# SSD mixer: the decays' differences on ScalarE, and SiLU as (1 + tanh(x/2)) x/2 ending in the projection's PSUM bank

## The chip, the core and the metric

The kernel runs on one core of a Trainium2 chip. The metric is the device time of one execution in microseconds, as a median of several runs. The profile is one further execution. Engines are called PE (TensorE), PEld (TensorE's weight loads), DVE (VectorE), ACT (ScalarE), POOL (GpSimd) and SP (SyncE, which here only issues DMAs). Each runs its own instructions in order; semaphores join them.

## The reference, cut to what matters

The program is a two-layer decoder of 1040 tokens (16 of them learned) and width 1024: a Mamba-2 mixer, a convolution network, a stick-breaking attention and a second convolution network. Only the mixer is changed:

```python
z, xbc, dt_raw = split(u @ w_in)                 # 2048, 2048 + 2*4*128, 32 columns
xbc = silu(causal_dwconv(xbc, conv_w, conv_b))   # 4 taps
xs, b_in, c_in = split(xbc)
dt = softplus(dt_raw + dt_bias);  a = -exp(a_log)
a_cs = cumsum(dt * a)                            # within a chunk
decay_in = exp(where(causal, a_cs[l] - a_cs[s], -inf))
y_diag = einsum(c_c, b_c, decay_in, x_c * dt)    # within a chunk
y_off  = einsum(c_c, state, exp(a_cs))           # from the state before it
y = y_diag + y_off + xs * d_skip
hg = rmsnorm_per_group(y * silu(z)) * gate_g
out = hg @ w_out
```

There are 4 groups of 8 heads with 64 columns each, and a state of 128. All is float32; a product is made of three matmuls of rounded parts (high × high, high × low, low × high: lines L156, L157, L158).

## The kernel before

**Tiles.** Channels lie on the 128 partitions, tokens along the free axis. The 1040 tokens are projected in three tiles j = 0, 1, 2 of 348, 348 and 344. A *block* is 128 columns of w_in. A projection tile is 24 matmuls (8 blocks of u, three parts each) into one PSUM bank `pj`: j = 0 and 1 rotate through the two banks of the pool mm, j = 2 has a bank of its own, `ex`, which the dt projection `dtr` also uses at the start. Three more banks are the pool sm (cb, pb, y, ms, and the small products of the dt path), two are the pool lg (px, S).

**A tile of xbc** (`in_block`, with `conv`): ACT makes the first tap from `pj` with weight and bias (L278), DVE adds three taps (L282, each reads `pj` and `xbc`), ACT applies Silu in SBUF (L465). The Silu isn't issued at once: it is put on the list `open`, which `settle` empties behind the next tile's L278. `pj` is free after the third tap.

**A tile of the gate** (`gate_group`): ACT applies Silu from `pj` to `z` (L497), and `pj` is free; DVE multiplies it into the rows y, which stand in the tiles named `xbc` (L504); ACT squares (L509, through `open`); DVE adds the squares of the group's four blocks (L513, L515). `gate_norm` then sums over partitions with a matmul (`ms`, L189), takes ln and exp on ACT (L192, L193, with a table load L180 ahead), refines on DVE (L194 to L197) and scales the four rows (L526). Where it runs, ACT changes its function table: natural logarithm and exp share one, Silu is in another.

**The loop of chunks.** The prologue (0 to about 112 us) transposes x, makes dt and projects group 0's six blocks; its order on the engines is set by the build's scheduler, from its own costs. From there to about 690 us the order is written out by hand. Each of 4 groups runs 9 chunks of 116 tokens (the last has 112). A chunk is: `ssd_front` (matmuls cb, px and pb; DVE masks cb into cbm, L601, makes xdt, L603, and multiplies the decays by cbm, L604; ACT copies bk, L610; POOL makes xde, L612); two to four projection tiles of blocks that come later; and `ssd_back` (matmuls S, L625, and y, L637 and L639; DVE adds the state, L632, and the four rows of y, L641, which frees y's bank). Groups 0 and 3 have 18 tiles to spread over 9 chunks, groups 1 and 2 have 30. These tiles are group g+1's inputs and group g's gate, and the norms of group g's gate stand between the tiles of the block behind it.

**The decays** (`ssd_decays`) run one step ahead, between a chunk's projection tiles: a DMA on SP's queue broadcasts the cumulated sums of 8 heads into D; DVE makes 8 instructions min(a_cs[l] − a_cs[s], 0), one for each head with its own column as scalar (L579); ACT takes the exp of all (L580); POOL scales the state's factors E by c (L583). The sums come from `dt_path`: ACT copies `dtr` (L401), transposes, softplus on DVE (a reciprocal, L418, and a series), cumulation by a matmul, a copy of the rows (L448) and DMAs to memory (L452), which D's DMA (L568) reads back.

Of the kernel before, what the change touches and what calls it, by code (L numbers as in the profile page):

```python
# [10 lines left out]
AF = mybir.ActivationFunctionType  # L11
ALU = mybir.AluOpType
# [10 lines left out]
TT = [(0, 348), (348, 348), (696, 344)]  # L23
TW = 352
QW = 1056
HALO = 4
# [43 lines left out]
class Trunk:  # L70
    def __init__(self, ctx, tc, a):
        self.tc, self.nc, self.a = tc, tc.nc, a
        nc = self.nc
        self.cp = ctx.enter_context(tc.tile_pool(name="cp", bufs=1))
        self.qp = ctx.enter_context(tc.tile_pool(name="qp", bufs=NQ))
        self.tmps = ctx.enter_context(tc.tile_pool(name="up", bufs=8))
        self.wp = ctx.enter_context(tc.tile_pool(name="wp", bufs=3))
        self.mp = ctx.enter_context(tc.tile_pool(name="mp", bufs=2, space=bass.MemoryType.PSUM))
        self.sp = ctx.enter_context(tc.tile_pool(name="sp", bufs=SMB, space=bass.MemoryType.PSUM))
        self.dp = ctx.enter_context(tc.tile_pool(name="dp", bufs=1, space=bass.MemoryType.DRAM))  # L80
        self.n = 0
        self.open = []
        self.consts()


# [29 lines left out]
    def consts(self):  # L115
        nc, cp = self.nc, self.cp
        self.params = cp.tile([P, NPAR], F32, tag="params", name="params")
        nc.gpsimd.dma_start(self.params, self.a["params"])
        self.ident = cp.tile([P, P], F32, tag="ident", name="ident")
        nc.gpsimd.memset(self.ident, 0.0)  # L120
        nc.gpsimd.affine_select(out=self.ident, in_=self.ident, compare_op=ALU.not_equal, fill=1.0, base=0,
                                pattern=[[-1, P]], channel_multiplier=1)
        self.one = cp.tile([P, 1], F32, tag="one", name="one")
        nc.vector.memset(self.one, 1.0)
        self.ones = cp.tile([P, P], F32, tag="ones", name="ones")
        nc.vector.memset(self.ones, 1.0)
        self.eps = cp.tile([P, 1], F32, tag="eps", name="eps")
        nc.vector.memset(self.eps, EPS)
        self.zero = cp.tile([P, HALO], F32, tag="zero", name="zero")
        nc.vector.memset(self.zero, 0.0)  # L130

        self.past = cp.tile([P, CB], F32, tag="past", name="past")
        nc.gpsimd.memset(self.past, 1.0)
        nc.gpsimd.affine_select(out=self.past, in_=self.past, compare_op=ALU.is_ge, fill=0.0, base=0,
                                pattern=[[1, CB]], channel_multiplier=-1)
# [135 lines left out]
            self.mm3(ps[:m, : halo + n], w[0][:, k * m : k * m + m], w[1][:, k * m : k * m + m], hi[:, o:e], lo[:, o:e], k == 0, k == kb - 1)  # L271
        return ps

    def conv(self, ps, out, n, taps, halo, wcol, bcol, between=lambda: None, last=None):

        nc = self.nc
        o = halo - taps + 1
        nc.scalar.activation(out, ps[:, o : o + n], AF.Identity, scale=wcol(0), bias=bcol)  # L278
        between()
        for i in range(1, taps):  # L280
            to = out if last is None or i + 1 < taps else last
            nc.vector.scalar_tensor_tensor(to, ps[:, o + i : o + i + n], wcol(i), out, op0=ALU.mult, op1=ALU.add)  # L282


    def load_x(self, pool, mx):
# [65 lines left out]
        for step, j in ORD:  # L351
            (scaled if step else stream)(j)
# [103 lines left out]
    def in_block(self, u, col, cv, out):  # L456

        nc = self.nc

        def tile(w, j):  # L460
            s0, n = TT[j]
            ps = self.project(w, u, j, HALO, bank=self.ex if j == 2 else None)
            t = out[0][:, s0 : s0 + n]
            self.conv(ps, t, n, 4, HALO, lambda i: self.par("ssd_conv_w", cv * 4 + i), self.par("ssd_conv_b", cv), self.settle)
            self.open.append(lambda: nc.scalar.activation(t, t, AF.Silu))  # L465

        return self.a["w_in"][col // P], tile

# [18 lines left out]
    def gate_group(self, u, g, x, acc, later):  # L487

        nc = self.nc
        tt = nc.vector.tensor_tensor  # L490

        def block(q):
            def tile(w, j):
                s0, n = TT[j]
                ps = self.project(w, u, j, 0, bank=self.ex if j == 2 else None)
                z = self.tmp("z")
                nc.scalar.activation(z[:, :n], ps[:, :n], AF.Silu)  # L497
                self.settle()
                later(j, lambda: product(j, z))

            def product(j, z):
                s0, n = TT[j]
                xq = x[q][:, s0 : s0 + n]
                tt(xq, xq, z[:, :n], op=ALU.mult)  # L504
                self.open.append(lambda: square(j, z))

            def square(j, z):
                s0, n = TT[j]
                nc.scalar.activation(z[:, :n], x[q][:, s0 : s0 + n], AF.Square)  # L509
                if q == 0:  # L510
                    acc[j] = z
                elif q == 1:
                    nc.vector.scalar_tensor_tensor(acc[j][:, :n], acc[j][:, :n], EPS * (DI // GROUPS) / P, z[:, :n], op0=ALU.add, op1=ALU.add)  # L513
                else:
                    tt(acc[j][:, :n], acc[j][:, :n], z[:, :n], op=ALU.add)  # L515

            return self.a["w_in"][4 * g + q], tile

        return [block(q) for q in range(4)]
# [8 lines left out]
    def settle(self):  # L528

        todo, self.open = self.open, []  # L530
        for f in todo:
            f()

    def stream(self, blocks, w0=None):


        calls = {}
        todo = []
        for src, f in blocks:
            if src is None:  # L540
                for j in range(3):
                    calls[3 * len(todo) + 1 + j] = lambda f=f, j=j: f(j)
            else:
                todo.append((src, f))
        w = [w0 or self.load_w(todo[0][0], D)]
        for n in range(3 * len(todo)):
            i, j = divmod(n, 3)
            if j == 0:
                if i + 1 < len(todo):
                    w.append(self.load_w(todo[i + 1][0], D))  # L550
                cur = w.pop(0)
            if n in calls:
                calls.pop(n)()
            todo[i][1](cur, j)
            yield
        self.settle()
        for f in calls.values():
            f()

    def ssd_decays(self, g, ct, c, pool):  # L560

        nc = self.nc
        h0 = GH * g
        t0, n = CH[c]
        cc = 3 * (c % 3) + c // 3
        dk = pool.tile([P, 1024], F32, tag="D", name=self.nm("D"))
        dk = dk[:n, : GH * CB].rearrange("p (h l) -> p h l", h=GH)
        nc.sync.dma_start(dk, self.acs_d[c, h0 : h0 + GH].unsqueeze(0).to_broadcast([n, GH, CB]))  # L568
        dk = dk[:, :, :n]
        ce = None  # L570
        if c:
            ce = pool.tile([P, GH * CB], F32, tag="E", name=self.nm("E"), bufs=2)
            ce = ce.rearrange("p (h l) -> p h l", h=GH)
            nc.sync.dma_start(ce, self.ea_d[c, h0 : h0 + GH].unsqueeze(0).to_broadcast([P, GH, CB]))
            ce = ce[:, :, :n]
        yield dk, ce

        for i in range(GH):
            nc.vector.tensor_scalar(dk[:, i], dk[:, i], self.cols[:n, 1, cc, h0 + i : h0 + i + 1], 0.0, op0=ALU.subtract, op1=ALU.min)  # L579
        nc.scalar.activation(dk, dk, AF.Exp)  # L580
        yield
        if c:
            nc.gpsimd.tensor_tensor(ce, ce, ct[:, t0 : t0 + n].unsqueeze(1).to_broadcast([P, GH, n]), op=ALU.mult)  # L583
        yield
# [287 lines left out]
    def up(self, layer, w0, forms, rest, pool):  # L872
# [7 lines left out]
        def block(b, t, w):  # L880
# [683 lines left out]
```

## Time and profile before

| what | us |
|---|---|
| time, median of 3 runs (lowest to highest) | 3022.47 (3021.38 to 3026.99) |
| the profiled execution's own time | 3024.83 |
| its span, first to last instruction | 3023.1 |
| busy PE, DVE, ACT, POOL | 2875.1, 2158.8, 1621.9, 1403.3 |
| PE busy, 0 to 110 / 110 to 690 / the rest | 94.68 / 554.62 / 2225.85 |
| mean granted clock of PE | 0.981 |

A row of a group reads: line, engine, operation, output<-inputs, sizes, count, then busy us, mean ns of one, and the idle time of the engine just before them with what ended it. A row of the timeline reads: start, length, engine, line, operation, and in brackets the idle time before it. Times count from the span's start.

### The profile page before, as it was taken

Reading aid. Unit: us, or ns where it says so; the run is one execution under the profiler, and the core shown is the slowest. Engines: PE = TensorE matmul, PEld = TensorE weight load, DVE = VectorE, ACT = ScalarE, POOL = GpSimd, SP = SyncE. Lnnn points to the kernel's source line nnn. Section 1 sums busy time; section 2 is a strip of 40 time slices with the busy share of each in tenths; the row PEclk is TensorE's granted clock in tenths of the full one; section 3 lists DMA queues with packets and bytes.
Section 4 is the critical chain, followed back from the end, with each engine's and each line's share of the span. In section 5 each row is a group of like instructions: output and inputs, shape, how many; then the busy total and the mean of one; then the engine's idle time right before and its main releaser. Section 6 shows DMA issues by size and latency. Waiting matters only on the chain.

```text
span 3023.1 us, 57199 instructions
## 1 busy us (share of the span) xinstructions
PE 2875.1 (95%) x21855; PEld 2733.1 (90%) x21855; DVE 2158.8 (71%) x3994; ACT 1621.9 (54%) x3308; POOL 1403.3 (46%) x1282
## 2 busy tenths in 40 slices
PE   7999999989989999998999999999997999998988
PEld 4998998889979999998998999999797999997778
DVE  5686868875376665568966888888748665568895
ACT  4555555553245555554334888877735555554432
POOL 1254444532415666658733222222234676667751
PEclk9999999999999999999999999999998999999999
DMA  5243323313222222243132222221331222225231
GB/s 161 75 118 86 109 78 111 113 53 139 74 78 64 78 80 77 84 160 132 47 117 72 60 65 65 68 59 52 129 112 64 85 76 79 77 84 176 91 105 56
DMA packets 125891, 272.76 MB, mean 90 GB/s; under 512 B 15888, under 2 KB 55440, under 8 KB 125616
## 3 DMA queue, kind: packets, MB, share of 16 engines
q1 hardware_dynamic: 120304, 258.17, 27.1%
q10 hardware_dynamic: 4048, 6.36, 0.6%
q0 software_dynamic: 1264, 4.57, 0.4%
q8 instruction: 172, 2.82, 0.4%
q14 instruction: 103, 0.84, 0.1%
HBM read 200.93 MB, written 53.21 MB: 84 GB/s over the span
## 4 chain that ended last, share of the span: by engine, by line
PE 52%; DVE 13%; ACT 4%; issue 3%; DMA 2%; POOL 0%; SPq 0%; DVEq 0%; ACTq 0%; POOLq 0%
PE p L156 9%; PE p L157 9%; PE p L158 9%; PE acc L157 4%; PE acc L156 4%; PE acc L158 4%; DVE gl L1007 3%; PE po L1314 2%; PE pj L156 2%; PE pj L158 2%; PE pj L157 2%; PE lg L1272 1%; DVE kp L1285 1%; PE wT L1299 1%; ACT kp L1275 1%
## 5 line engine op out<-in xcount | busy, mean ns | idle before, releaser
L156 PE MATMUL pj<-uh,wh 128*128 128x348 f32 (+2 forms) x1536 | 507.3, 331 | 16.1 <-DVE qs L1223 7.1
L157 PE MATMUL pj<-ul,wh 128*128 128x348 f32 (+2 forms) x1536 | 498.7, 325 | 0.0
L158 PE MATMUL pj<-uh,wl 128*128 128x348 f32 (+2 forms) x1536 | 496.2, 323 | 0.0
L157 PE MATMUL p<-bl,fh 128*128 128x262 f32 (+1 forms) x1408 | 401.0, 285 | 14.0 <-DVE bl L827 14.0
L156 PE MATMUL p<-bh,fh 128*128 128x262 f32 (+1 forms) x1408 | 401.3, 286 | 4.2 <-ACT fh L858 3.5
L158 PE MATMUL p<-bh,fl 128*128 128x262 f32 (+1 forms) x1408 | 399.3, 284 | 0.0
L859 POOL TENSOR_TENSOR fl<-x,fh 128x1024 fp32r<-128x1024 f32 x88 | 212.7, 2418 | 306.4 <-ACT fh L858 277.5
L150 POOL TENSOR_TENSOR wl<-w,wh 128x1024 fp32r<-128x1024 f32 (+2 forms) x80 | 164.6, 2060 | 327.1 <-ACT wh L149 327.0
L156 PEld LDWEIGHTS pj<-uh,wh 128*128 128x128 f32 x1536 | 292.0, 190 | 23.8 <-DVE qs L1223 9.2
L157 PE MATMUL p<-bl,wh 128*128 128x262 f32 (+1 forms) x1056 | 301.8, 286 | 8.5 <-DVE bl L827 8.5
L156 PE MATMUL p<-bh,wh 128*128 128x262 f32 (+1 forms) x1056 | 301.9, 286 | 6.3 <-ACT bh L826 6.3
L158 PE MATMUL p<-bh,wl 128*128 128x262 f32 (+1 forms) x1056 | 301.2, 285 | 0.0
L157 PEld LDWEIGHTS pj<-ul,wh 128*128 128x128 f32 x1536 | 292.6, 190 | 1.4 <-issue 0.5
L158 PEld LDWEIGHTS pj<-uh,wl 128*128 128x128 f32 x1536 | 291.9, 190 | 0.3 <-issue 0.2
L157 PEld LDWEIGHTS p<-bl,fh 128*128 128x128 f32 x1408 | 268.0, 190 | 16.1 <-DVE bl L827 15.9
L282 DVE SCALAR_TENSOR_TENSOR c<-p,params,c 128x260 f32<-128x260 f32 (+1 forms) x440 | 207.9, 481 | 94.4 <-ACT c L278 92.6
L156 PEld LDWEIGHTS p<-bh,fh 128*128 128x128 f32 x1408 | 268.4, 191 | 6.0 <-ACT fh L858 3.9
L158 PEld LDWEIGHTS p<-bh,fl 128*128 128x128 f32 x1408 | 267.4, 190 | 0.1
L157 PE MATMUL acc<-gl,wh 128*128 128x260 f32 (+1 forms) x672 | 217.9, 326 | 19.8 <-DVE gl L1007 19.8
L909 DVE TENSOR_TENSOR p<-p,ft 128x262 f32<-128x262 f32 (+1 forms) x176 | 76.8, 436 | 221.6 <-ACT ft L906 128.9
L384 DVE TENSOR_TENSOR h<-h,acc 128x256 f32<-128x256 f32 (+4 forms) x232 | 102.6, 450 | 175.1 <-PE acc L158 172.5
L156 PE MATMUL acc<-gh,wh 128*128 128x260 f32 (+1 forms) x672 | 215.0, 325 | 8.7 <-DVE p L1054 5.4
(309 smaller groups left out, 8539.4 us busy)
## 6 DMA issues: line engine op xcount, KB each, us to landing
w<-in_w_up SPq DMA_DIRECT2D x88, 512.0 KB
w<-in_w_down SPq DMA_DIRECT2D x44, 512.0 KB
w<-in_w_in SPq DMA_DIRECT2D x40, 512.0 KB
E<-ea_d SPq DMA_DIRECT2D x32, 464.0 KB
D<-acs_d SPq DMA_DIRECT2D x32, 420.5 KB
g<-c SPq DMA_DIRECT2D x88, 130.0 KB
g<-c SPq DMA_DIRECT2D x88, 128.0 KB
b<-g SPq DMA_DIRECT2D x16, 520.0 KB
```

The lines of the kernel that those rows point to most:

```text
L150: nc.gpsimd.tensor_tensor(wl[:, :n], w32[:, :n], wh[:, :n].bitcast(F32), op=ALU.subtract)
L156: mm(out, wh, uh, start=first, stop=False, skip_group_check=joins)
L157: mm(out, wh, ul, start=False, stop=False, skip_group_check=joins)
L158: mm(out, wl, uh, start=False, stop=last, skip_group_check=joins)
L282: nc.vector.scalar_tensor_tensor(to, ps[:, o + i : o + i + n], wcol(i), out, op0=ALU.mult, op1=ALU.add)
L384: self.nc.vector.tensor_tensor(h[f][:, o], h[f][:, o], ps[:, :n], op=ALU.add)
L859: tt(lo[:, :n], t, hi[:, :n].bitcast(F32), op=ALU.subtract)
L909: add = lambda o, x, y: tt(o[:, :N], x[:, :N], y[:, :N], op=ALU.add)
L1007: tt(gl, x, gh.bitcast(F32), op=SUB)
L1272: nc.tensor.matmul(ps[:nt, :m], part[:, c0 : c0 + nt], ks[a][:, s0 : s0 + m], start=x == 0, stop=x == 1)
L1275: nc.scalar.activation(kp[:nt, :m], ps[:nt, :m], AF.Sigmoid, scale=self.rt[2][:nt, i : i + 1])
L1314: nc.tensor.matmul(po[64 * a : 64 * a + 64, w], v[: CH[c][1], c, 64 * a : 64 * a + 64], wt[a][: CH[c][1], c, :nt], start=x == 0, stop=x == ...
```

## The change

1. `ssd_decays`: the 8 DVE instructions become 8 ACT instructions Relu(a_cs[s] − a_cs[l]), with the head's column as bias and a scale of −1, and the exp takes a scale of −1. The value is the same.
2. SiLU becomes (1 + tanh(x/2)) · x/2. Tanh is in one table with exp. For xbc the halving is in the parameters: taps and biases of the convolution are multiplied by 0.5 once at the start (one DVE instruction). The last tap now writes back into the bank `pj`; ACT takes the tanh of it into a temporary; DVE makes (th + 1) · pj into the row. `pj` is free after that.
3. The gate: ACT takes tanh(z/2) from `pj`; DVE makes (th + 1) · pj into `pj` (for group 3 into the temporary); the product with the rows, with a factor of 0.5, reads it there. `pj` is free after the product, not after ACT.
4. A second list, `next`, holds DVE's SiLU step and the sums of squares; `follow` empties it behind the next tile's first tap.

```diff
@@ consts
+        halves = self.par("ssd_conv_b", 0, 24 + 24 * 4)
+        nc.vector.tensor_scalar(halves, halves, 0.5, None, op0=ALU.mult)
@@ conv
             nc.vector.scalar_tensor_tensor(to, ps[:, o + i : o + i + n], wcol(i), out, op0=ALU.mult, op1=ALU.add)
+            if i == 1:
+                behind()
@@ in_block
-            t = out[0][:, s0 : s0 + n]
-            self.conv(ps, t, n, 4, HALO, lambda i: self.par("ssd_conv_w", cv * 4 + i), self.par("ssd_conv_b", cv), self.settle)
-            self.open.append(lambda: nc.scalar.activation(t, t, AF.Silu))
+            t, y = out[0][:, s0 : s0 + n], ps[:, HALO : HALO + n]
+            self.conv(ps, t, n, 4, HALO, lambda i: self.par("ssd_conv_w", cv * 4 + i), self.par("ssd_conv_b", cv), self.settle, y, self.follow)
+
+            def silu():
+                th = self.tmp("th")[:, :n]
+                nc.scalar.activation(th, y, AF.Tanh)
+                self.next.append(lambda: nc.vector.scalar_tensor_tensor(t, th, 1.0, y, op0=ALU.add, op1=ALU.mult))
+
+            self.open.append(silu)
@@ gate_group
-                z = self.tmp("z")
-                nc.scalar.activation(z[:, :n], ps[:, :n], AF.Silu)
+                th = self.tmp("z")
+                nc.scalar.activation(th[:, :n], ps[:, :n], AF.Tanh, scale=0.5)
                 self.settle()
-                later(j, lambda: product(j, z))
+                self.follow()
+                z = th if g == 3 else ps
+                nc.vector.scalar_tensor_tensor(z[:, :n], th[:, :n], 1.0, ps[:, :n], op0=ALU.add, op1=ALU.mult)
+                later(j, lambda: product(j, z, th))
...
-                tt(xq, xq, z[:, :n], op=ALU.mult)
-                self.open.append(lambda: square(j, z))
+                nc.vector.scalar_tensor_tensor(xq, z[:, :n], 0.5, xq, op0=ALU.mult, op1=ALU.mult)
+                self.open.append(lambda: square(j, th))
...
                 nc.scalar.activation(z[:, :n], x[q][:, s0 : s0 + n], AF.Square)
+                self.next.append(lambda: add(j, z))
@@ ssd_decays
         for i in range(GH):
-            nc.vector.tensor_scalar(dk[:, i], dk[:, i], self.cols[:n, 1, cc, h0 + i : h0 + i + 1], 0.0, op0=ALU.subtract, op1=ALU.min)
-        nc.scalar.activation(dk, dk, AF.Exp)
+            nc.scalar.activation(dk[:, i], dk[:, i], AF.Relu, scale=-1.0, bias=self.cols[:n, 1, cc, h0 + i : h0 + i + 1])
+        nc.scalar.activation(dk, dk, AF.Exp, scale=-1.0)
```

In the changed kernel the lines are a little lower: the tap is L284, the tanh of xbc L472, its SiLU step L473, the taps' first step L280, Relu and exp L603 and L604, the gate norm's scaling L543. Three places show how the order moves; each row has the line, the operation and the tiles with their numbers.

DVE in the prologue, before: pj_596 is the first block's tile j = 2, in the bank `ex`, pj_728 the next tile that uses it. Rows from the reciprocal on:

```order
L418 RECIPROCAL dt_641<-dt_641 116x288
L282 SCALAR_TENSOR_TENSOR xbc_536<-pj_596,params,xbc_536 128x344
L419 TENSOR_TENSOR dt_642<-dt_640,dt_641 116x288
L282 SCALAR_TENSOR_TENSOR xbc_536<-pj_596,params,xbc_536 128x344
L282 SCALAR_TENSOR_TENSOR xbc_774<-pj_775,params,xbc_774 128x348
L420 TENSOR_TENSOR dt_640<-dt_642 116x288
L282 SCALAR_TENSOR_TENSOR xbc_536<-pj_596,params,xbc_536 128x344
L282 SCALAR_TENSOR_TENSOR xbc_774<-pj_775,params,xbc_774 128x348
```

The same place now; pj_599 and pj_737 are the two tiles, pj_673 and pj_705 the second block's other two:

```order
L422 RECIPROCAL dt_646<-dt_646 116x288
L284 SCALAR_TENSOR_TENSOR xbc_537<-pj_599,params,xbc_537 128x344
L423 TENSOR_TENSOR dt_647<-dt_645,dt_646 116x288
L284 SCALAR_TENSOR_TENSOR xbc_537<-pj_599,params,xbc_537 128x344
L284 SCALAR_TENSOR_TENSOR xbc_672<-pj_705,params,xbc_672 128x348
L424 TENSOR_TENSOR dt_645<-dt_647 116x288
L284 SCALAR_TENSOR_TENSOR pj_599<-pj_599,params,xbc_537 128x344
L284 SCALAR_TENSOR_TENSOR xbc_672<-pj_705,params,xbc_672 128x348
L425 TENSOR_SCALAR dt_646<-dt_645 116x288
L284 SCALAR_TENSOR_TENSOR pj_705<-pj_705,params,xbc_672 128x348
L473 SCALAR_TENSOR_TENSOR xbc_537<-th_699,pj_599 128x344
```

The last reader of the bank was a tap that stood six rows behind the reciprocal; now it is the SiLU step, ten rows behind it. On PE pj_728 came 39 matmuls of other tiles after pj_596's last; pj_737 comes 17 after pj_599's last.

ACT at the prologue's end, before, around the first chunk's decays:

```order
L278 ACTIVATE xbc_983<-pj_984,params 128x348
L465 ACTIVATE xbc_886<-xbc_886 128x348
L149 ACTIVATE wh_1076<-w_143_1074 128x1024
L580 ACT_TABLE_LOAD
L580 ACTIVATE D_1174<-D_1174 116x928
L278 ACTIVATE xbc_886<-pj_947,params 128x344
L465 ACT_TABLE_LOAD
L465 ACTIVATE xbc_983<-xbc_983 128x348
```

And now:

```order
L453 ACTIVATE ea_888<-rows_884 96x348
L472 ACTIVATE th_930<-pj_850 128x344
L280 ACTIVATE xbc_903<-pj_904,params 128x348
L603 ACTIVATE D_1211<-D_1211,cols 116x116 x8
L472 ACTIVATE th_962<-pj_904 128x348
L280 ACTIVATE xbc_903<-pj_936,params 128x348
L604 ACTIVATE D_1211<-D_1211 116x928
```

The Relus, which read D after its DMA, stand ahead of the tanh of pj_904, whose SiLU step frees its bank for pj_1007; before, only the exp stood there on ACT, and on DVE the differences stood ahead of the last tap of pj_984, which freed that tile's bank.

DVE in group 1's loop, at the end of the second norm of group 0's gate (its last two of eight steps), before: pj_2982 is the third tile of the block around it.

```order
L526 SCALAR_TENSOR_TENSOR xbc_774<-xbc_774,params,y_2971 128x348
L526 SCALAR_TENSOR_TENSOR xbc_886<-xbc_886,params,y_2971 128x348
L282 SCALAR_TENSOR_TENSOR xbc_2847<-pj_2982,params,xbc_2847 128x344 x3
L194 TENSOR_TENSOR z_2385<-y_3025 128x344
L195 TENSOR_TENSOR z_2385<-z_2385,ms_3023 128x344
```

And now; pj_2979 is that block's second tile, pj_3069 its third:

```order
L543 SCALAR_TENSOR_TENSOR xbc_785<-xbc_785,params,y_3058 128x348
L543 SCALAR_TENSOR_TENSOR xbc_903<-xbc_903,params,y_3058 128x348
L284 SCALAR_TENSOR_TENSOR xbc_2932<-pj_3069,params,xbc_2932 128x344
L473 SCALAR_TENSOR_TENSOR xbc_2932<-th_3095,pj_2979 128x348
L284 SCALAR_TENSOR_TENSOR xbc_2932<-pj_3069,params,xbc_2932 128x344
L284 SCALAR_TENSOR_TENSOR pj_3069<-pj_3069,params,xbc_2932 128x344
```

The SiLU step of the second tile, which frees its bank, stands behind the whole norm and the third tile's first tap; before, that bank was free after the tile's own third tap, ahead of the norm.

More of the change, by code (lines that the diff above doesn't have):

```diff
@@ L81, in __init__ @@
         self.n = 0
-        self.open = []
+        self.open, self.next = [], []
         self.consts()
@@ L272, in project, with conv @@
         return ps
-    def conv(self, ps, out, n, taps, halo, wcol, bcol, between=lambda: None, last=None):
+    def conv(self, ps, out, n, taps, halo, wcol, bcol, between=lambda: None, last=None, behind=lambda: None):
         nc = self.nc
@@ L495, in tile, with product @@
                 ps = self.project(w, u, j, 0, bank=self.ex if j == 2 else None)
-                z = self.tmp("z")
-                nc.scalar.activation(z[:, :n], ps[:, :n], AF.Silu)
+                th = self.tmp("z")
+                nc.scalar.activation(th[:, :n], ps[:, :n], AF.Tanh, scale=0.5)
                 self.settle()
-                later(j, lambda: product(j, z))
-            def product(j, z):
+                self.follow()
+                z = th if g == 3 else ps
+                nc.vector.scalar_tensor_tensor(z[:, :n], th[:, :n], 1.0, ps[:, :n], op0=ALU.add, op1=ALU.mult)
+                later(j, lambda: product(j, z, th))
+            def product(j, z, th):
                 s0, n = TT[j]
                 xq = x[q][:, s0 : s0 + n]
-                tt(xq, xq, z[:, :n], op=ALU.mult)
-                self.open.append(lambda: square(j, z))
+                nc.vector.scalar_tensor_tensor(xq, z[:, :n], 0.5, xq, op0=ALU.mult, op1=ALU.mult)
+                self.open.append(lambda: square(j, th))
             def square(j, z):
@@ L509, in square, with add @@
                 nc.scalar.activation(z[:, :n], x[q][:, s0 : s0 + n], AF.Square)
+                self.next.append(lambda: add(j, z))
+            def add(j, z):
+                n = TT[j][1]
                 if q == 0:
@@ L530, in settle, with follow @@
         todo, self.open = self.open, []
+        for f in todo:
+            f()
+    def follow(self):
+        todo, self.next = self.next, []
         for f in todo:
@@ L556, in stream @@
         self.settle()
+        self.follow()
         for f in calls.values():
```

## The prediction

> **What bounds the kernel now.** First I read the busy time by stage, over the three parts of the program (columns: stretch, its length, busy us and instructions of PE, PEld, DVE, ACT, POOL, the granted TensorE clock, DMA).
>
> ```profile
> 0.00:110.00 110.00, 94.68 (x521) 71.58 (x522) 61.74 (x125) 57.51 (x101) 19.79 (x35) 1.00 0.42 130
> 110.00:690.00 580.00, 554.62 (x4023) 516.26 (x4021) 451.89 (x918) 307.49 (x447) 258.92 (x146) 0.98 0.33 97
> ...
> ```
>
> TensorE sets the end in both. In the loop of chunks (110 to 690) it is idle for 580 − 554.62 = 25.4 us; ScalarE, with 307, and VectorE, with 452, are far from full. An edit on these two engines pays only through those 25 us and through the clock. What TensorE waited for there, from the view of waits (total us, times, longest):
>
> ```profile
> PE pb L608 <- DVE z L195: 6.9, 3, 2.6
> PE ms L189 <- ACT bk L610: 6.5, 3, 5.7
> PE pj L156 <- ACT bk L610: 4.9, 2, 3.2
> PE S L625 <- POOL xde L612: 3.3, 4, 1.2
> ```
>
> The clock, from the same kind of windows around three of these waits:
>
> ```profile
> 297.50:300.10 2.60, 0.04 (x2) 0.00 (x1) 2.46 (x6) 2.31 (x3) 2.60 (x2) 0.97 0.96 225
> 300.10:307.00 6.90, 6.53 (x20) 5.75 (x21) 6.76 (x16) 2.52 (x4) 0.29 (x1) 0.52 0.35 123
> 307.00:314.00 7.00, 7.00 (x44) 6.80 (x43) 6.86 (x10) 5.57 (x8) 4.47 (x2) 1.00 0.00 0
> ...
> 457.00:460.40 3.40, 3.40 (x14) 3.40 (x13) 3.33 (x7) 1.20 (x3) 0.00 (x0) 0.50 0.30 101
> ...
> 484.30:491.00 6.70, 5.54 (x19) 5.57 (x20) 6.56 (x15) 4.05 (x9) 3.25 (x2) 0.50 0.09 37
> ...
> 627.70:637.90 10.20, 4.47 (x14) 3.72 (x14) 9.64 (x26) 4.67 (x6) 1.85 (x1) 0.50 0.01 5
> ```
>
> At full clock a matmul takes 7.00/44 = 0.16 us, so a tile of 24 takes 3.9. After a wait of some 2.5 us or more the clock is halved for 3.4 to 10.2 us: 27.2 us in these four places, half of it lost. The ceiling of a gain in the loop is thus 25.4 + 13.6 = 39 us.
>
> **Removed from ScalarE's path.** Its longest wait, and one place where it reaches TensorE (timeline: start, length, then in brackets the idle time before and its releaser):
>
> ```profile
> ACT D L580 <- DVE D L579: 110.7, 36, 7.8
> ```
>
> ```profile
> 477.30 2.21 POOL L583 TENSOR_TENSOR E<-E,xbc 128x928 f32<-128x928 f32 x1
> 477.91 4.01 DVE L579 TENSOR_SCALAR D<-D,cols 116x116 f32<-116x116 f32 x8
> 481.95 0.98 ACT L580 ACTIVATE D<-D 116x928 f32<-116x928 f32 x1 [7.82 <-DVE D L579]
> 482.84 0.63 ACT L278 ACTIVATE xbc<-pj,params 128x348 f32<-128x348 f32 x1
> 483.50 1.81 DVE L282 SCALAR_TENSOR_TENSOR xbc<-pj,params,xbc 128x348 f32<-128x348 f32 x3 [1.58 <-ACT xbc L278]
> 485.46 0.63 PE L156 MATMUL pj<-uh,wh 128*128 128x352 f32 x1 [3.23 <-ACT bk L610]
> ```
>
> The differences ran long beside POOL's E, the exp waited for them, the convolution's first step stood behind the exp, and its taps freed the bank that TensorE wanted. (The view names the copy bk; the bank's last reader is the tap, which ended at 485.31.) With the differences on ScalarE this chain is gone: 3.23 us, and half of 6.7, so −6.6 in group 2; in group 1 its twin of 1.66 us (shown further down), which cost no clock.
>
> **Busy time moved.**
>
> ```profile
> L579 DVE TENSOR_SCALAR D<-D,cols 116x116 f32<-116x116 f32 x256 | 80.8, 387 | 4.7 <-DMA D<-acs_d 4.7
> L504 DVE TENSOR_TENSOR xbc<-xbc,z 128x348 f32<-128x348 f32 x32 | 42.1, 1316 | 7.7 <-ACT z L497 7.7
> L282 DVE SCALAR_TENSOR_TENSOR xbc<-pj,params,xbc 128x348 f32<-128x348 f32 x118 | 68.1, 578 | 34.1 <-ACT xbc L278 31.3
> L580 ACT ACT_TABLE_LOAD x36 | 46.2, 1283 | 2.5 <-DMA D<-acs_d 1.9
> L580 ACT ACTIVATE D<-D 116x928 f32<-116x928 f32 x32 | 31.4, 980 | 95.1 <-DVE D L579 95.1
> L610 ACT ACTIVATE bk<-pb 116x128 f32<-116x128 f32 x32 | 8.5, 264 | 2.9 <-PE pb L608 2.8
> L497 ACT ACTIVATE z<-pj 128x348 f32<-128x348 f32 x32 | 14.7, 460 | 37.5 <-PE pj L158 37.4
> L1173 ACT ACTIVATE wh<-w,params 128x128 fp32r<-128x128 f32 x168 | 55.9, 457 | 0.0
> ```
>
> In the loop VectorE loses the differences (80.8 us in these 256), and the gate product, an operation on two SBUF tensors that averages 1.3 us, now reads PSUM as the tap does: 32 × 0.58 = 18.5 for 42.1. Added are 54 SiLU steps and 48 of the gate, priced as the tap too: 102 × 0.58 = 59. VectorE's 452 become about 406. ScalarE gains 288 Relus: between the copy bk (0.26) and the copy with a pointer (0.46) I take 0.31 back to back, 2.5 us for a chunk's eight, so 36 × 2.5 = 90 us; of the loads the order keeps 35 where the trace has 110, which returns 75 × 1.283 = 96. Both engines stay off the bound, so none of it counts by itself. The eight Relus and the exp make 2.5 + 1.0 = 3.5 us in ScalarE's queue, and behind them stands a tile's first convolution step; a mixer bank is wanted again two tiles after its own, 7.8 us, and the SiLU that now frees it waits for the next tile's matmuls, its first step and, side by side, the tanh (0.46, as L497) and the next tile's first tap: 3.9 + 0.63 + 0.58 + 0.58 = 5.7 us. So this late release costs nothing while ScalarE is less than 2.1 us late. Halving the parameters' columns is one small step at the start, under the wait for x.
>
> The Trainium skill (ScalarE: Activation LUTs, Rules for kernel authors) sends relu, max and min to VectorE, which speaks against moving them; by What ACT_TABLE_LOAD costs an ACTIVATE with a pointer takes 280 ns + 0.833 a column, by estimate 3.0 us for the eight, and a switch about 2.7 us instead of the row's 1.28. By these ScalarE would save 200 − 109 = 91 us instead of 6, still off the bound; the trace disagrees about the switch, since L465's load of 1.28 us began at 483.48 and its function followed it at 484.78.
>
> **Added in the prologue.** There the order, not a duration, is the change.
>
> ```profile
> 79.55 1.95 DVE L418 RECIPROCAL dt<-dt 116x288 f32<-116x288 f32 x1
> ...
> 100.63 0.52 DVE L448 COPY rows<-rows 96x348 f32<-96x348 f32 x1 [2.60 <-PE rows L446]
> ...
> 111.84 2.10 DVE L579 TENSOR_SCALAR D<-D,cols 116x116 f32<-116x116 f32 x8 [4.69 <-DMA D<-acs_d]
> ```
>
> ```profile
> 114.58 0.40 PE L156 MATMUL pj<-uh,wh 128*128 128x352 f32 x1 [1.62 <-DVE xbc L282]
> ```
>
> (a) The copies of dtr, which free the bank that the first block's third tile uses, come later on ScalarE, and 15 transposes stand alone on TensorE: where 9 matmuls lay between them before and 20 ahead of the last six. Without this cover of 1.4 to 4.6 us each set waits for its splits; an estimate of +2 us (0 to 3.5). (b) The second block's third tile stands 29 matmuls (4.7 us) behind the transposes of dt, and its bank waits for a SiLU behind the reciprocal and ten more steps, by estimate 7.4 us (1.95 and ten near the tap's 0.58 or a little under it), which begin 2 us after those transposes: 4.7 us idle, and as a wait above 2.5 us it brings a half clock, 3.4 lost: +8.1 (2 to 9). (c) D arrived 111.84 − 100.63 = 11.2 us after the copy of the rows. Now the Relus that wait for it stand before a tanh whose SiLU frees a bank wanted 72 matmuls, 11.6 us, after the transposes of the rows: 11.2 + 0.5 + 2.5 + 0.46 + 0.58 = 15.2, so 3.6 idle for the 1.62 of before, and 1.7 to 3.4 of clock: +4.2 (2 to 6). Sum +14 (4 to 18).
>
> The Trainium skill (TensorE: Matmul & The Clock Gate, Part 1) has the half rate only after an idle window of about 3.4 us, free-running. Here 2.6 us was enough, against it; by the page (a) and (c) might miss it, and the sum would be 12.
>
> **Gate norms in the loops of groups 1 and 2.** Each has three, between tiles of the next block.
>
> ```profile
> 308.27 0.52 DVE L194 TENSOR_TENSOR z<-y 128x348 f32<-128x348 f32 x1
> ...
> 310.48 4.20 DVE L526 SCALAR_TENSOR_TENSOR xbc<-xbc,params,y 128x348 f32<-128x348 f32 x4
> 314.60 1.79 DVE L282 SCALAR_TENSOR_TENSOR xbc<-pj,params,xbc 128x344 f32<-128x344 f32 x3
> ```
>
> ```profile
> 312.56 0.32 PE L156 MATMUL pj<-uh,wh 128*128 128x352 f32 x1
> ...
> 329.54 0.40 PE L156 MATMUL pj<-uh,wh 128*128 128x352 f32 x1 [1.66 <-ACT bk L610]
> ```
>
> In the new order the SiLU of the block's second tile stands behind the second norm and the next tap: 314.60 + 0.58 + 0.58 = 315.8 at the earliest, where TensorE took that bank for the tile after next at 312.56. That is 3.2 us idle, and 1.7 of clock; the SiLU of the first tile delays the first norm's followers by 0.6. Twice 5.5 = +11, between 0 (the norm not stretched, 2.06 as in group 3 instead of 4.20, and an earlier start) and 14. Less 1.66 and 6.6 from above: +3.
>
> **Group 3 and xde.**
>
> ```profile
> 624.48 2.47 DVE L194 TENSOR_TENSOR z<-y 128x348 f32<-128x348 f32 x1
> 628.46 2.06 DVE L526 SCALAR_TENSOR_TENSOR xbc<-xbc,params,y 128x348 f32<-128x348 f32 x4
> 632.50 0.98 ACT L580 ACTIVATE D<-D 116x928 f32<-116x928 f32 x1 [6.12 <-DVE D L579]
> 633.70 1.53 PE L189 MATMUL ms<-z,ones 128*128 128x348 f32 x2 [5.73 <-ACT bk L610]
> ```
>
> Here bk stood behind the exp, and it behind the differences and a norm. Free of that, the wait of 5.73 shrinks to about 1.6, and of the 5.1 us of clock some 4 return: −8 (−12 to −4). The four waits on xde (3.3) go with VectorE's lighter load: −3 (−3.3 to 0).
>
> **Sum.** 14 + 3 − 8 − 3 = +6 us against the profiled execution's 3024.8 (its span 3023.1), which stands 2.4 above the median: 3030.8 there. I add 1 for the convolution network's entry, where a few tiles are ordered anew with no row to price them (−3 to 3): 3029 as a median beside 3022.5.
>
> **Rivals.** *Faster.* The prologue's order costs only its lower bound, 4, and the norm is not stretched, so the SiLU is in time; all of 1.66 + 6.6 goes, with 12 in group 3 and 3.3 at xde: 4 − 8.3 − 12 − 3.3 = −19.6, 3003. For it: every large wait of the loop leads through the exp or a stretched op. Against: the order of (b) and of the norms. It decides where (b) falls below 2 us. *About even.* The two sums meet, at 3019 to 3028. *Banks.* D arrives late in one chunk of three, ScalarE passes the slack of 2.1 us, and 12 chunks lose 2 us each: 3029 + 24 = 3053. Against: D waited for its DMA once in the whole loop. *The change doesn't do it:* tanh, exp and Relu still reload. Then 75 loads return to a ScalarE that has 270 us free, and the time would be as forecast within 3.
>
> **Chances.** Slower (the forecast) 0.43, its own range 3021 to 3046, of which 0.04 falls within 6 us of before; faster 0.34; even 0.18; banks 0.04; not as said 0.01, which I count with the forecast. Less than 0.2%, 6 us, can't be told from no change. The range, 3000 to 3046, runs from just past the faster case to the dear ends of (b), (c) and the norms. Faster by over 0.2%: 0.34; within: 0.04 + 0.18 = 0.22; slower: 0.44.
>
> **What would show it.** Right: a wait of 3 us or more of the third tile of block 2 in the prologue with a clock of 0.5 behind it, the next stage entered 8 us or more late, waits of pj on the SiLU line near 313 and 470, and none on xde. Wrong: the prologue as before, or clocks of 1.00 from 480 to 640 with the norms' waits gone; then it is faster. Table loads should be 35, L579's group gone from VectorE, and the loop's VectorE time near 400.

## The result: 0.3% slower, as forecast

The changed kernel takes 3033.91 us (median of 7 runs, 3029.81 to 3037.33) against 3022.13 (7 runs of the kernel before beside it): a ratio of 1.003, 95% interval 1.0021 to 1.004 (the two medians alone give 1.0039). The forecast was 3029, from 3000 to 3046. The profiled execution took 3035.01 us with a span of 3033.3, 10.2 above the span of before. In the experiments below one run of sbuf_loop (7179.45 us) and one of loads_back (13307.43 us) were in a slow state and are left out of their times.

**The stages after.** The first view to read is again the busy time by stage:

```profile
0.00:60.00 60.00, 45.42 (x214) 24.35 (x215) 32.51 (x68) 27.83 (x53) 12.31 (x31) 1.00 0.58 191
60.00:110.00 50.00, 43.60 (x237) 40.42 (x236) 29.93 (x61) 18.78 (x37) 7.38 (x4) 0.86 0.14 41
110.00:690.00 580.00, 557.46 (x4034) 521.94 (x4034) 382.58 (x733) 292.45 (x656) 249.39 (x137) 0.97 0.33 94
```

VectorE has 69 us less in the loop (382.58 for 451.89), ScalarE 15 less, and the clock in the second half of the prologue is 0.86, where it was 1.00. These stretches are fixed in time, and the changed kernel is some 14 us later in its work when the last of them begins. Over the whole program TensorE runs the same 21855 matmuls, now 2885.9 us busy for 2875.1, at a mean clock of 0.977 for 0.981. What it waited for from 110 to 690:

```profile
PE pj L158 <- DVE xbc L473: 11.2, 3, 4.1
PE pb L632 <- DVE z L197: 4.7, 2, 2.4
PE y L661 <- DVE D L628: 4.4, 1, 4.4
PE ms L191 <- ACT bk L634: 1.6, 3, 0.8
...
PE S L649 <- POOL xde L636: 0.3, 1, 0.3
```

Against the rows of before: ms behind bk fell from 6.5 to 1.6, S behind xde from 3.3 to 0.3, pj behind bk from 4.9 to nothing. A new wait of 11.2 took their place, on the SiLU step L473 that now frees the bank.

**The prologue.** TensorE's waits there, from the timeline, and the clock around them:

```profile
66.65 0.60 PE L323 MATMUL xT<-ident,x 128*128 128x128 f32 x3 [0.47 <-DVE ul L264]
67.54 1.13 PE L323 MATMUL xT<-ident,x 128*128 128x128 f32 x6 [0.30 <-DVE ul L264]
69.34 1.18 PE L323 MATMUL xT<-ident,x 128*128 128x128 f32 x6 [0.66 <-DVE ul L264]
70.97 0.66 PE L158 MATMUL pj<-uh,wh 128*128 128x348 f32 x1 [0.45 <-ACT rows L405]
...
86.50 0.66 PE L158 MATMUL pj<-uh,wh 128*128 128x348 f32 x1 [4.52 <-DVE xbc L473]
```

```profile
66.00:71.00 5.00, 3.12 (x18) 1.75 (x16) 4.91 (x12) 4.50 (x13) 0.00 (x0) 0.92 0.02 7
71.00:82.00 11.00, 10.99 (x51) 10.57 (x51) 5.02 (x11) 3.17 (x6) 1.69 (x1) 0.72 0.00 0
82.00:86.80 4.80, 0.29 (x1) 0.30 (x2) 4.80 (x11) 1.91 (x4) 0.70 (x1) 0.70 0.31 109
86.80:90.00 3.20, 3.20 (x12) 3.20 (x12) 3.06 (x8) 0.00 (x0) 0.00 (x0) 0.50 0.02 5
...
117.00:120.20 3.20, 0.23 (x1) 0.24 (x2) 0.80 (x2) 3.20 (x11) 0.00 (x0) 1.00 0.63 161
120.20:125.00 4.80, 4.80 (x22) 4.80 (x22) 3.54 (x7) 2.37 (x4) 2.39 (x1) 0.64 0.26 102
```

The bank `ex` came free 4.52 us late, and 12 matmuls then took 3.2 us, where full clock would make it 1.9. Before that, behind the four short waits, 51 matmuls took 11 us. The third wait, of the first chunk's D (ScalarE first, then VectorE, then TensorE):

```profile
116.65 2.36 ACT L603 ACTIVATE D<-D,cols 116x116 f32<-116x116 f32 x8 [6.79 <-DMA D<-acs_d]
118.92 0.44 ACT L472 ACTIVATE th<-pj 128x348 f32<-128x348 f32 x1
119.39 0.52 DVE L473 SCALAR_TENSOR_TENSOR xbc<-th,pj 128x348 f32<-128x348 f32 x1 [7.68 <-ACT th L472]
119.97 0.43 PE L158 MATMUL pj<-uh,wh 128*128 128x352 f32 x1 [3.08 <-DVE xbc L473]
```

The eight Relus took 2.36 us; one convolution tile's tanh stood behind them, its SiLU step behind that, and the bank behind the step.

**The norms in the loops of groups 1 and 2.**

```profile
325.29 4.04 DVE L543 SCALAR_TENSOR_TENSOR xbc<-xbc,params,y 128x348 f32<-128x348 f32 x4
329.25 0.56 DVE L284 SCALAR_TENSOR_TENSOR xbc<-pj,params,xbc 128x344 f32<-128x344 f32 x1
329.74 0.50 DVE L473 SCALAR_TENSOR_TENSOR xbc<-th,pj 128x348 f32<-128x348 f32 x1
330.30 0.66 PE L158 MATMUL pj<-uh,wh 128*128 128x352 f32 x1 [4.15 <-DVE xbc L473]
```

This is the chain that the prediction drew from the order: stretched norm, next tile's tap, SiLU step, bank. Its twin in group 2 is a wait of 3.95 us at 489.84.

**Where the time went, place by place.** In both traces the start of a chunk's cb matmul marks the same point of the program. The table gives its start in the changed kernel less that before, both counted from their first matmul (an example: the second chunk's cb starts at 155.08 after and at 140.39 before; the first matmul is 0.5 us later there):

| point of the program | us behind before | step |
|---|---|---|
| after the prologue (from the second chunk to the end of group 0) | 14.2 | +14.2 |
| after the norms in group 1's loop | 17.7 | +3.5 |
| after the norms in group 2's loop | 18.0 | +0.3 |
| group 3, ahead of the last chunk but one | 14.8 | −3.2 |
| the last chunk's cb | 5.9 | −8.9 |
| first matmul of the output projection | 10.9 | +5.0 |
| end | 9.7 | −1.2 |

### The profile page after: what moved, and what is told of

It is laid out like the page before. It is cut to its first block, busy times and chain, and to the rows that moved or that the text cites. A ratio compares the mean times of both kernels' runs of the same rounds, so it can differ in the third digit from the quotient of the medians.

```text
span 3033.3 us, 57175 instructions
## 1 busy us (share of the span) xinstructions
PE 2885.9 (95%) x21855; PEld 2743.4 (90%) x21855; DVE 2098.4 (69%) x3827; ACT 1602.7 (53%) x3521; POOL 1395.6 (46%) x1282
## 5 line engine op out<-in xcount | busy, mean ns | idle before, releaser
L158 PE MATMUL pj<-uh,wh 128*128 128x348 f32 (+2 forms) x1536 | 510.0, 332 | 24.2 <-DVE xbc L473 15.7
L284 DVE SCALAR_TENSOR_TENSOR c<-p,params,c 128x260 f32<-128x260 f32 (+1 forms) x440 | 208.3, 482 | 93.3 <-ACT c L280 91.2
```

The source lines that it names most:

```text
L158: mm(out, wh, uh, start=first, stop=False, skip_group_check=joins)
```

## The experiments

The theory, A: the change gains by taking the differences off VectorE, and loses more by ending the SiLU in the bank, which is then free only after the tanh and the step on VectorE. Rival B: the Relus burden ScalarE. Rival C: the shared table is the gain, and the form in SBUF would lose to GpSimd what the bank had saved. Times below are medians; ratios are against the kernel before on the same chip, with their 95% interval.

### Each half alone, and the SiLU ending in SBUF

**decays_only** is the kernel before with the edit of `ssd_decays` alone:

```diff
-            nc.vector.tensor_scalar(dk[:, i], dk[:, i], self.cols[...], 0.0, op0=ALU.subtract, op1=ALU.min)
-        nc.scalar.activation(dk, dk, AF.Exp)
+            nc.scalar.activation(dk[:, i], dk[:, i], AF.Relu, scale=-1.0, bias=self.cols[...])
+        nc.scalar.activation(dk, dk, AF.Exp, scale=-1.0)
```

> The kernel before with part 1 alone: Relu and exp on ScalarE, the Silu function kept, so that a tap frees the bank as before and the prologue's order on TensorE is that of before. Theory A (the change loses by the bank's late release, and gains by the differences leaving VectorE): the gains without the loss. The wait of 1.62 us at 113 goes, 1.7 and 3.2 + 3.4 in the loops of groups 1 and 2, some 9 in group 3, 1 to 3 on xde: 3022 - 19 = 3003 (2998 to 3011). Theory B (the eight Relus, 90 us more for ScalarE, are what costs): 3022 or more. Table loads stay at 110.

3009.95 us, 0.9954 (0.9942 to 0.9967): 12 to 14 us faster than before. It lies within the expected range, 7 us above its centre. B is out: the Relus don't cost more than they gain. The prologue stays near where it was (1.5 us behind at the second chunk).

**tanh_only** is the change with that edit undone, so that the differences are on VectorE.

> The change without part 1: tanh and the bank form kept, the differences on VectorE. Theory A: the losses without the gains. The prologue has the changed order, +14 us, the norms' tiles wait for the SiLU step, +11, and the exp waits for VectorE as before: 3022 + 25 = 3047 (3038 to 3055). Theory B: without the Relus the loss is gone, 3022 or less.

3047.57 us, 1.008 (1.0066 to 1.0094), at the expected sum. The prologue is 11 us behind and the norms add 12, with seven waits of pj on L473:

```profile
PE pj L158 <- DVE xbc L473: 18.0, 7, 5.0
...
PE pb L632 <- DVE z L197: 7.4, 2, 3.7
PE ms L191 <- ACT bk L634: 7.0, 3, 6.3
```

The wait of ms behind bk, 6.3 us, is back as in the kernel before (5.7). With the differences on ScalarE the longest is 0.8 in the change and 2.6 in decays_only, so most of it comes with the differences on VectorE.

**sbuf_all** is the change with one place different: the last tap, the tanh and the SiLU step use the row in SBUF.

```diff
-            t, y = out[0][:, s0 : s0 + n], ps[:, HALO : HALO + n]
+            t = out[0][:, s0 : s0 + n]
+            y = t
```

> The change with one difference: the convolution's last tap writes to the row in SBUF, the tanh and the SiLU step read it there, and the bank is free after the third tap as before; tanh, the shared table, the lists and the decays on ScalarE stay. Theory A: the prologue's wait of 4.5 us and its clock go, and so do the two waits of 4 us in the loops with theirs: 3034 - 13 - 11 = 3010 (3003 to 3017). Theory B: no change from 3034, since the Relus are there. Theory C (the SiLU step on two SBUF tensors is stretched beside POOL and costs what the bank had saved): 3030 or more.

3003.76 us, 0.9935 (0.9922 to 0.9949): 30 us less than the change and 20 less than before, from this one place. The waits on the SiLU step are gone from the prologue and the loop, and the order of the prologue is near that of before. The price that C named is real but lies beside the path: the SiLU step reads two SBUF tensors, and averages 736 and 1081 ns where in the bank it took 508 and 505. First the change, then this kernel:

```profile
L473 DVE SCALAR_TENSOR_TENSOR xbc<-th,pj 128x348 f32<-128x348 f32 x42 | 21.3, 508 | 9.8 <-ACT th L472 9.8
...
L473 DVE SCALAR_TENSOR_TENSOR xbc<-th,pj 128x344 f32<-128x344 f32 x21 | 10.6, 505 | 4.2 <-ACT th L472 4.2
```

```profile
L474 DVE SCALAR_TENSOR_TENSOR xbc<-th,xbc 128x348 f32<-128x348 f32 x41 | 30.2, 736 | 5.1 <-ACT th L473 4.8
...
L474 DVE SCALAR_TENSOR_TENSOR xbc<-th,xbc 128x344 f32<-128x344 f32 x21 | 22.7, 1081 | 4.1 <-ACT th L473 3.7
```

That is 21 us more of VectorE for 30 us less of the program. The Trainium skill (SBUF — State Buffer, Who interferes with whom) says that a VectorE instruction with two SBUF inputs contends with a GpSimd instruction that reads SBUF. The trace agrees: in sbuf_all's timeline from 130 us on, every such step longer than 0.6 us has arithmetic of GpSimd beside it, and those without take 0.51.

**sbuf_prologue** does it in group 0's six blocks alone (`y = t if cv in (0, 1, 2, 3, 16, 20) else ps[...]`), **sbuf_loop** in all others.

> As the one before, but only in the six blocks of group 0, which the prologue projects; the loop's tiles end in the bank as in the change. Theory A: the prologue's 14 us come back but for 1 or 2, the loop's waits of 4 us stay: 3034 - 13 = 3021 (3016 to 3026). Theory B: 3034.

3019.09 us, 0.9982 (0.9974 to 0.9991): 15 less than the change. At the second chunk it is 0.9 us ahead of before, where the change was 14.2 behind; the loop keeps its two waits (9.0 us in all).

> The other half of ending in SBUF: only the loop's blocks, while group 0's six in the prologue end in the bank. If the losses of prologue and loop add, 3034 - (3019 - 3004) = 3019 (3015 to 3023), with the prologue's wait of 4.5 us on the SiLU step still there and no wait on it after 120 us. If the loop's waits were a consequence of the prologue's late start, 3030 or more.

3021.04 us, 0.9995 (0.9986 to 1.0004): 13 less than the change, with the prologue 13.7 us behind as expected. TensorE waits for no SiLU step after 120 us. The two halves add: 15 + 13 = 28 for the 30 of both. In the loop the order is the change's own, written by hand, so the 13 us are the bank's earlier release. In the prologue the scheduler's order moves with the form, and these runs don't divide the 15 us between order and release.

### Is it the place in the order, or the bank?

**flush_before_norm** keeps the bank form and empties both lists ahead of a norm, so that the SiLU step no longer stands behind it:

```diff
             if n in calls:
+                self.settle()
+                self.follow()
                 calls.pop(n)()
```

> The change, with both lists emptied ahead of each gate norm, so that the tanh and the SiLU step of the tile before stand ahead of the norm on ScalarE and VectorE; they still end in the bank. If the place behind the norm makes the two waits of TensorE of 4.15 and 3.95 us in the loops of groups 1 and 2, they go, with the half clocks behind them: 3034 - 8 - 5 = 3021 (3018 to 3026). If the bank form itself costs there, wherever the step stands (VectorE now waits for the tanh ahead of the norm), 3030 or more. The prologue's loss stays in both.

3033.65 us, 1.0041 (1.0027 to 1.0054): no better than the change. The expectation of 3021 was wrong. The two large waits of pj did go, but pb now waits as long. On ScalarE the tanh stands ahead of the norm's table load, ln and exp, and waits for the last tap; VectorE waits for the tanh, then for the norm's exp (ScalarE, VectorE, TensorE):

```profile
312.92 0.46 ACT L472 ACTIVATE th<-pj 128x348 f32<-128x348 f32 x1 [3.05 <-DVE pj L284]
313.40 1.28 ACT L182 ACT_TABLE_LOAD   x1
...
313.42 0.52 DVE L473 SCALAR_TENSOR_TENSOR xbc<-th,pj 128x348 f32<-128x348 f32 x1 [0.53 <-ACT th L472]
315.71 0.52 DVE L196 TENSOR_TENSOR z<-y 128x348 f32<-128x348 f32 x1 [1.78 <-ACT y L195]
...
316.84 0.47 PE L634 MATMUL pb<-ident,xbc 128*116 128x128 f32 x1 [4.46 <-DVE z L197]
```

In the change that wait was 2.39 us. So a different place for the step doesn't help by itself: the wait moves from the bank to the norm. This run can't tell place from bank, since a tanh ahead of the norm would delay it in either form. sbuf_loop can: there the step keeps its place behind the norm, the bank is free after the tap, and the two waits are gone.

**sbuf_all_gate** writes the gate's (th + 1) z to the temporary for all groups (`z = th`), which frees the gate's bank a step earlier.

> Ending in SBUF for the gate too: (th + 1) z goes into the temporary for all groups, so that the gate's bank is free a step earlier and the product reads two SBUF tensors. The gate's late release was costed at nothing; if that is right, 3004 (3000 to 3008), a little above where GpSimd stretches the product. If the gate's bank was late somewhere, 2 to 8 us less.

3007.1 us, 0.9948 (0.9935 to 0.996), no difference from 3003.76 that the intervals can tell. Beside the SBUF form the gate's late release costs nothing; the prediction's sum had no term for it.

### What table loads cost

**loads_back** puts a load of the table that holds Silu ahead of each chunk's Relus, so that the exp must load again: 111 loads.

```diff
+        nc.scalar.preload_act_table_set("silu_and_others")
         for i in range(GH):
             nc.scalar.activation(dk[:, i], dk[:, i], AF.Relu, ...)
```

> The change with a load of another function table ahead of each chunk's Relus, so that the exp has to load its own again: 111 loads instead of 35, near the 110 of before, 98 us more of ScalarE. If the loads lie off the path, 3034 to 3038: what ScalarE does for a chunk grows from 3.4 to 6 us, so single tiles may be late. If the shared table is what the change gains by, 3050 or more.

3050.04 us (3 runs), 1.0094 (1.0079 to 1.011): 16 us slower than the change (18 in the next two expectations). I had favoured 0 to 4; it is at the 3050 that the expectation gave to the shared table as the gain. **loads_look** is the same kernel, run once more for its profile.

> The kernel with 76 table loads put back once more, for its profile; it was 18 us slower than the change. If the longer block of Relus and exp passes the slack of about 2 us that the bank form leaves, the waits of pj on the SiLU step (11.2 us in the loop of the change) grow by some 10 us in several places between 120 and 690, and half clocks with them.

3048.82 us. The waits of pj on the step are 17.1 us in prologue and loop together, for 15.7 in the change: the expectation missed again. What grew are pb behind the norm's L197 (9.8 for 4.7) and ms (5.3 for 0.6 behind VectorE, 4.6 for 1.6 behind bk). Up to the thirteenth chunk it runs with the change (13.7 and 14.2 us behind before); the loss comes at the norms in the loops of groups 1, 2 and 3.

**sbuf_loads** is the same edit where the SiLU ends in SBUF.

> The same 76 loads put back where the SiLU step ends in SBUF and a tap frees the bank. If the 18 us came from the bank's hold, ScalarE has more slack here and it costs little: 3004 + 0 to 6. If loads cost wherever they stand, 3004 + 18 = 3022.

3027.47 us, 1.0013 (1.0004 to 1.0021): 24 us slower than sbuf_all, and above both figures of the expectation. So the loads don't cost by the bank's hold. Here TensorE waits 4.62 us at a norm, where sbuf_all's longest such wait is 2.4, and ScalarE's rows ahead of it show why:

```profile
297.37 1.28 ACT L603 ACT_TABLE_LOAD   x1
298.67 2.37 ACT L605 ACTIVATE D<-D,cols 116x116 f32<-116x116 f32 x8
301.06 1.28 ACT L606 ACT_TABLE_LOAD   x1
302.35 0.98 ACT L606 ACTIVATE D<-D 116x928 f32<-116x928 f32 x1
...
304.18 0.62 ACT L280 ACTIVATE xbc<-pj,params 128x348 f32<-128x348 f32 x1
304.71 0.48 ACT L523 ACTIVATE z<-xbc 128x344 f32<-128x344 f32 x1
305.20 1.28 ACT L182 ACT_TABLE_LOAD   x1
306.49 0.46 ACT L194 ACTIVATE y<-ms 128x348 f32<-128x348 f32 x1
306.99 0.49 ACT L195 ACTIVATE y<-y 128x348 f32<-128x348 f32 x1
```

```profile
310.07 0.47 PE L634 MATMUL pb<-ident,xbc 128*116 128x128 f32 x1 [4.62 <-DVE z L197]
```

In the plain chunks the loads cost nothing at all: up to the thirteenth this kernel is 2.1 us behind sbuf_all throughout, from the prologue, and in 27 of the 35 steps from one chunk to the next the distance doesn't grow. Beside a gate norm, where ScalarE's ln and exp stand in the chain to TensorE, a chunk with two loads more delays them. ScalarE has 56% of the span busy and is still the path there.

These runs price loads at two places, ahead of the Relus and ahead of the exp. They don't price the shared table against the kernel before, whose loads stand elsewhere: decays_only has 110 loads and ran in 3009.95. What the change gains by sharing the table is not shown.

### The cell that was left, and the last chunk

**sbuf_dve** is sbuf_all with the differences on VectorE.

> The SiLU ending in SBUF, with the shared table, but the differences on VectorE: the cell that is left of decays (VectorE, ScalarE) by SiLU (Silu function, tanh in the bank, tanh in SBUF). The decays on ScalarE gained 14 us beside the Silu function and 14 beside the bank form. If they add, 3004 + 14 = 3018 (3013 to 3023); the tanh form in SBUF by itself is then worth some 5 us against before.

3030.81 us, 1.0026 (1.0016 to 1.0036); expected were 3018. All six cells, medians in us:

| differences on | Silu function | tanh, ending in the bank | tanh, ending in SBUF |
|---|---|---|---|
| VectorE | 3022.1 (before) | 3047.6 | 3030.8 |
| ScalarE | 3010.0 | 3033.9 (the change) | 3003.8 |

Down the columns the move of the differences gains 12, 14 and 27 (14, 15 and 27.5 by the ratios, since the medians are from several sets of runs): it doesn't add with the SBUF form. The tanh form brings new steps to VectorE, and with the differences there too it is VectorE that is late at the norms (pb waits 3.70 and 3.71 us and ms 7.1, where sbuf_all has at most 2.4 and 0.8). That this makes the 27 is read from the waits, not isolated. From the Silu function to the tanh in the bank costs 25 and 24 us, whichever engine has the differences; to the tanh in SBUF costs 8 or gains 6.

**sbuf_pool** is sbuf_all with the output projection's first twelve differences moved to GpSimd; three of them stand on VectorE ahead of the last chunk's state.

```diff
-            ops = [self.split(..., "y") for q in range(4)]
+            ops = [self.split(..., "y", self.nc.gpsimd if g == 0 else None) for q in range(4)]
```

> The change ending in SBUF everywhere, and the low parts of the output projection's first group, three wide differences that stand on VectorE ahead of the last chunk's state, moved to GpSimd, which is idle there. The last chunk's y waited 4.6 us for VectorE, with a half clock behind it. If those 1.4 us were in that chain, 3004 - 1.4 to - 5 = 2999 to 3002; if the stretched norm ahead of them sets it, 3004.

3007.26 us, 0.9952 (0.9939 to 0.9964), no gain. The wait of y stayed (4.3 us for 4.6), but not because the three were off its chain: in both kernels VectorE runs without a gap from the norm to the product D that y waits for. On GpSimd they stood beside the norm's scaling, which took 5.83 us instead of 3.77, so the 1.4 us that left VectorE's queue came back as 2.1. First sbuf_all, then this kernel:

```profile
625.29 3.77 DVE L544 SCALAR_TENSOR_TENSOR xbc<-xbc,params,y 128x348 f32<-128x348 f32 x4
```

```profile
624.85 5.83 DVE L544 SCALAR_TENSOR_TENSOR xbc<-xbc,params,y 128x348 f32<-128x348 f32 x4
...
626.74 3.56 POOL L169 TENSOR_TENSOR yl<-y,yh 128x348 fp32r<-128x348 f32 x3
```

## Why the prediction was right, step by step

- *The bound.* Right: the engines' 84 us less of busy time in the loop paid only where TensorE had waited. From the second chunk to the thirteenth the two kernels keep the same distance, 14.2 us.
- *The differences' chain.* Right. The wait of 3.23 us of group 2 and its twin are gone, and decays_only shows 12 to 14 us for the move as a whole, group 3 and xde included.
- *"None of it counts by itself" of ScalarE's loads.* Wrong as a general sentence. It holds in the plain chunks; 76 loads put back cost 16 and 24 us, most of it at the norms. The forecast had no such term, and how much of the measured time hangs on it stays open.
- *Eight Relus at 2.5 us:* 2.36. The 3.0 us that the prediction worked out from the Trainium skill (ScalarE: Activation LUTs, What ACT_TABLE_LOAD costs) left out that section's overlap of about 93 ns between back-to-back instructions; with it the same formula gives an estimate of 2.4, and the trace agrees. *VectorE near 400 in the loop:* 382.6, for the 406 of the working. That had taken out 256 of the 288 differences (80.8 of 92.9 us) and made only 32 of the 48 gate products shorter, and the gate's own step takes 0.51 where it was priced at 0.58.
- *Prologue, +14 us:* +14.2, with the terms shared out otherwise. (a) The waits of the transposes and of the bank behind them sum to 0.47 + 0.30 + 0.66 + 0.45 = 1.9 us as estimated, but brought a half clock that I hadn't priced, some 3 us (51 matmuls in 11.0 us, for 8.2). (b) The wait was 4.52 for 4.7, and the clock behind it cost some 2 instead of 3.4 (0.50 over 3.20 us and 0.90 over the next 3.5), as the slow clock had begun in the wait itself (0.70 over 82.0 to 86.8). (c) 3.08 for 3.6, and 1.7 of clock (0.64 over 4.80 us). The errors cancel, one of 3 up and two of 1 to 2 down, so that the sum came out to 0.2 us is in part luck.
- *Gate norms, +3:* +3.8 (3.5 and 0.3). The waits were 4.15 and 3.95 for 3.2, by the same chain. By the starts of the chunks, 5.9 and 6.8 us were lost there and 2.4 and 6.5 returned behind it: 12.7 for the 11 of the forecast, 8.9 for its 8.3. The forecast named 313 and 470 as their places; with the prologue's delay and the tiles between, they began at 326 and 486.
- *Group 3, −8, and xde, −3:* −8.9 and −3.2.
- *Not foreseen:* the last chunk. Its y waited 4.40 us for D where 1.46 stood before, and the clock was halved behind it, +5.0 in all. That, with the sum of +6 otherwise met (14.2 + 3.8 − 3.2 − 8.9 = 5.9), is where 3029 falls short of 3034. In the rows ahead of it group 3's second norm is stretched, which had not been so before:

```profile
649.24 2.59 DVE L199 TENSOR_TENSOR y<-y,z 128x348 f32<-128x348 f32 x1
651.86 4.57 DVE L543 SCALAR_TENSOR_TENSOR xbc<-xbc,params,y 128x348 f32<-128x348 f32 x4
...
665.25 1.09 DVE L628 TENSOR_TENSOR D<-D,cbm 112x896 f32<-112x896 f32 x1
```

```profile
648.97 2.48 POOL L152 TENSOR_TENSOR wl<-w,wh 128x1024 fp32r<-128x1024 f32 x1
651.42 1.31 POOL L655 TENSOR_TENSOR state<-state,cd 128x512 f32<-128x512 f32 x1
652.70 2.38 POOL L607 TENSOR_TENSOR E<-E,xbc 128x896 f32<-128x896 f32 x1
```

  In the kernel before the two took 0.52 and 2.06, so they are 4.6 us longer beside GpSimd's three instructions. There it was the third norm that was stretched, by 1.8 us (its L197 took 2.29), so 2.8 us are new. sbuf_pool supports this cause, since more of GpSimd's work beside the scaling made it longer still; no run takes GpSimd's work away from it.
- *The rivals.* "Faster" would have needed (b) below 2 us; it was 4.52 and its clock. It came true once the bank was free after the tap. "Banks" needed D to be late in one chunk of three; ScalarE waited for its DMA once, for the first chunk. "The change doesn't do it" is out with 35 loads.
- *The range.* It reached from the faster case to the dear ends, and the chance of a slower kernel was put at 0.44. The place-by-place sums are better evidence for the mechanism than the range is.

## What to carry to other kernels

A fused last step that writes into PSUM hands the bank's release to the slowest reader: count what is queued ahead of that reader on each engine, and where the bank is wanted next. Here a form that was slower on its own engine, by 21 us, made the program 30 us faster. An engine at half load can still be the path at one recurring spot (the gate norms), so price a saving there and not by its share; and where a scheduler orders part of the program, read the new order before anything else, since order and late release together moved 14 us here.

## What the runs showed that I had not expected

- The half clock needed no single long gap. Four waits of 0.30 to 0.66 us within 66 to 71 (TensorE busy for 3.12 of 5.00 us) were followed by a clock of 0.72 over the next 11 us. In the kernel before, a lone wait of 1.62 us left it at 1.00. The Trainium skill (TensorE: Matmul & The Clock Gate, Part 1) ties the half rate to an idle window of some 3.4 us; these rows show a stretch that was busy by more than half. What share decides can't be told from them.
- Table loads of 1.28 us each cost nothing in the plain chunks; 76 of them cost 16 to 24 us, most of it beside the norms.
- The gain of an edit depended on the other: 12, 14 or 27 us for the same move of the differences.
